# A weight-gradient matmul: where the halved output stores stand, and on which queues

## The chip, the cores and the metric

The kernel runs on one core of one Trainium2 chip. The metric is the device time of one execution in microseconds (us). The core has TensorE (PE in the profile, its weight loads PEld), VectorE (DVE), ScalarE (ACT), GpSimd (POOL) and SyncE (SP). SP, ACT and POOL can also issue DMA transfers, each on a queue of its own; the transfers run on 16 DMA engines.

## The reference

```python
batch, m, k, n = 16, 512, 1024, 768
grad_weight = np.einsum('bmk,bmn->kn', input, grad_output)   # float32 in and out
```

With batch and m taken together this is one product of a 1024 x 8192 matrix (X transposed) with an 8192 x 768 one (G); the result is 1024 x 768 floats, 3.1 MB.

## The kernel before, in words

The 8192 rows come in as 32 units of 256 rows, loaded by GpSimd and converted to bf16 on the way (lines 153 to 160). Only the first tiles are loaded as float32, by SP (L128, L130) and ScalarE (L129, L131), and rounded on VectorE and ScalarE (L202).

The result is cut in halves both ways: K into 0..511 and 512..1023, N into 0..383 and 384..767. Block A is the upper left quarter, B the upper right, C the lower left, D the lower right. Each has four pieces, q = 0 to 3, of 128 x 384 elements. The first four tiles are multiplied directly. For the other units a scheme with seven products in place of eight is used (Strassen's, in a form with few additions): the blocks 1, 5, 6, 7 are products of sums of quarters, made by VectorE (L184 to L198), and are added into A to D at the end. Running sums stand in SBUF (`acc` for A to D, `macc` for 1, 5, 6, 7) and visit PSUM banks: `fill` copies a sum into a bank (L309, ScalarE), `multiply` adds matmuls to it (L331), `close` brings it back (L356 on ScalarE; L360 to L378 on VectorE).

`PLAN` is a long string that fixes the order on TensorE, VectorE, ScalarE and GpSimd: `B2.1` is one matmul for block B, q = 2; `vB2` closes it on VectorE, `cC0` on ScalarE; `qA0` adds the shared block to A0 on GpSimd (L388, `add_shared`) and stores it; `pC1` adds it without a store. SP is not among the engines with a fixed order: the framework's scheduler orders the DMAs on SP's queue when the program is built.

Every piece of A to D is stored once, by `store` (L285 to L291): sixteen stores, all in the last 13 us, all issued by SP. A store of a piece is 128 rows of 384 floats (1536 bytes), 192 KB; half of one is 128 rows of 768 bytes, 96 KB. `stores[0]` counts the stores in the order of PLAN, and `HALVED = 4` makes the first four go out in two halves, one behind the other on SP. The end of PLAN, which holds most of the last sums:

```python
"51.2 vB3 f52@0 51.1 C0.1 pC1 C0.1 fB0@4 v51 C0.2 fB2@5 C1@2.4 vC0 B1.2 52.1 vC1 52.2 vB1 B2.3 v52 B2.2 "
"B0.4 vB2 B0.2 vB0 "
```

The last four stores are those of `vB1` (B1), `v52` (which also completes D2, L366 and L368), `vB2` (B2) and `vB0` (B0).

Before the first data arrive, TensorE runs dummy products (`WARMUP`, L134 to L142), all into one PSUM bank.

Of the kernel before, what the change touches and what calls it, by code (L numbers as in the profile page):

```python
# [9 lines left out]
P = 128  # L10
# [65 lines left out]
).split()  # L76

WARMUP = [("b", 512), ("f", 512), ("f", 512)] + 14 * [("b", 128)]
PAIRS_HELD = 11
SUMS_HELD = 8  # L80
MERGED = 2
HALVED = 4
ASIDES = 7
RESIDENT = 3
FOLDED = True
# [3 lines left out]
def kernel(  # L89
# [6 lines left out]
    nc = tc.nc  # L96
    bf16 = mybir.dt.bfloat16
    f32 = mybir.dt.float32
# [4 lines left out]
    NH = N // 2  # L103
# [4 lines left out]
    X = input.rearrange("b m k -> (b m) k")  # L108
    G = grad_output.rearrange("b m n -> (b m) n")
    OUT = out.rearrange("(ks p) n -> p ks n", p=P)  # L110
# [5 lines left out]
    psum = ctx.enter_context(tc.tile_pool(name="psum", bufs=1, space=bass.MemoryType.PSUM))  # L116
# [9 lines left out]
    xf = [pairs.tile([P, K], f32, name=f"xf{s}", tag="xp") for s in range(2)]  # L126
# [1 line left out]
    nc.sync.dma_start(out=gf[:, LEFT], in_=G[0:P, LEFT])  # L128
    nc.scalar.dma_start(out=xf[0], in_=X[0:P, :])  # L129
    nc.sync.dma_start(out=gf[:, RIGHT], in_=G[0:P, RIGHT])  # L130
    nc.scalar.dma_start(out=xf[1], in_=X[P : 2 * P, :])  # L131

    wps = psum.tile([P, 512], f32, name="bank7")
    for dt, cols in WARMUP:  # L134
        dtype = f32 if dt == "f" else bf16
        nc.tensor.matmul(
            wps[:, 0:cols],
            nc.const_aps.tensor(1.0, (P, P), dtype),
            nc.const_aps.tensor(1.0, (P, cols), dtype),
            start=True,  # L140
            stop=True,
        )  # L142
# [103 lines left out]
    def sum_of(p, q):  # L246
        if p in SLOT:
            return macc[:, SLOT[p], q, :]
        row = q if p in "AB" else Q + q
        return acc[:, row, LEFT if p in "AC" else RIGHT]  # L250
# [7 lines left out]
    prepared = set()  # L258
    opened = {(p, q): [] for p in streams for q in range(Q)}
    stores = [0]  # L260
# [21 lines left out]
    def last(p, q):  # L282
        return done[p, q] == len(streams[p])

    def store(p, q, c0, c1, engine):  # L285
        row = q if p in "AB" else Q + q
        at = 0 if p in "AC" else NH
        cuts = [c0, (c0 + c1) // 2, c1] if stores[0] < HALVED else [c0, c1]
        stores[0] += 1
        for d0, d1 in zip(cuts, cuts[1:]):  # L290
            engine.dma_start(out=OUT[:, row, at + d0 : at + d1], in_=sum_of(p, q)[:, d0:d1])  # L291

    asides = {(p, q): [] for p in streams for q in range(Q)}
    free_asides = list(range(ASIDES))
# [46 lines left out]
    def close(engine, p, q, queue):  # L341
        parts, carried = opened[p, q].pop(0)
        final = last(p, q) and not opened[p, q] and p not in ("1D" if FOLDED else "1")
        dst = sum_of(p, q)
        away = engine == "c" and not carried
        if away:
            assert not last(p, q)
            asides[p, q].append(free_asides.pop(0))
            dst = aside[:, asides[p, q][-1], :]
        for tile_, at, c0, c1 in parts:  # L350
            b = tile_[:, at : at + c1 - c0]
            to = dst[:, c0:c1]
            if engine == "c":
                assert carried or away
                assert not final or p in "ABC"
                nc.scalar.copy(out=to, in_=b)  # L356
            elif engine == "k":
                assert carried and not final and last("D", q) and not opened["D", q]
                d = sum_of("D", q)[:, c0:c1]
                (nc.vector.tensor_add if p == "C" else nc.vector.tensor_sub)(out=to, in0=b, in1=d)  # L360
                folded.add((p, q))
            elif final and p == "5":
                assert carried and {("6", q), ("7", q)} <= closed
                nc.vector.tensor_sub(out=to, in0=b, in1=sum_of("6", q)[:, c0:c1])  # L364
                d = sum_of("D" if FOLDED else "6", q)[:, c0:c1]
                nc.vector.tensor_sub(out=d, in0=b, in1=sum_of("7", q)[:, c0:c1])  # L366
                if FOLDED:
                    store("D", q, c0, c1, queue)  # L368
            elif final and (p, q) not in prepared:
                assert carried and (SHARED[p], q) in closed and (p != "D" or ("5", q) in closed)  # L370
                nc.vector.tensor_add(out=to, in0=b, in1=sum_of(SHARED[p], q)[:, c0:c1])  # L371
                if p in "BCD" and len(parts) == 2:
                    store(p, q, c0, c1, nc.sync if c0 == 0 else nc.scalar)
            elif carried:
                assert (p, q) not in prepared
                nc.vector.tensor_copy(out=to, in_=b)  # L376
            else:
                nc.vector.tensor_add(out=to, in0=b, in1=to)  # L378
        if final and p in "ABCD" and engine == "v" and (len(parts) == 1 or p == "A"):
            store(p, q, 0, NH, queue)  # L380
        if last(p, q) and not opened[p, q] and not (engine == "c" and p in "ABC"):
            closed.add((p, q))
        spilled.add((p, q))

# [12 lines left out]
    for token in PLAN:  # L397
        op, rest = token[0], token[1:]
        if op in "xg":
            stage, u = rest.split(".")  # L400
            (sum_x if op == "x" else sum_g)(int(stage), int(u))
        elif op == "r":
            round_by(*ROUNDINGS[int(rest)])
        elif op == "f":
            block, banks = rest.split("@")
            fill(block[0], int(block[1]), [int(b) for b in banks.rstrip("s").split("+")], banks.endswith("s"))
        elif op in "cvk":
            close(op, rest[0], int(rest[1]), nc.scalar if rest[2:] == "a" else nc.sync)
        elif op in "pq":
            add_shared(rest[0], int(rest[1]), op == "p", nc.scalar if rest[2:] == "a" else nc.sync)  # L410
        else:
            block, n = token.split(".")
            block, _, where = block.partition("@")
            multiply(block[0], int(block[1]), where, int(n))
# [34 lines left out]
```

## Time and profile before

| What | Value |
|---|---|
| Median of 3 runs | 161.4 us (161.18 to 161.44) |
| Profiled execution: its own time | 161.48 us |
| Profiled execution: span in the profile | 159.7 us |
| TensorE busy | 154.6 us (97%) |
| VectorE busy | 136.1 us (85%) |
| ScalarE busy | 104.4 us (65%) |
| GpSimd busy | 42.6 us (27%) |
| Granted TensorE clock | 0.999 |
| Stores: 12 of 192 KB, 8 of 96 KB | 2.1 and 1.7 us from issue to landing (medians) |

The span runs from the first to the last instruction of the profile; the execution's own time is 1.78 us longer. Times in the views are in us from the start of the span. L12 is line 12 of the kernel before.

### The profile page before, as it was taken

The numbers are of one execution on the slowest core, as the hardware profiler recorded it, in microseconds if no ns is written. First come the engines' busy times: TensorE is split into PE (matmuls) and PEld (weight loads), VectorE is DVE, ScalarE is ACT, GpSimd is POOL, SyncE is SP. The second block draws the span as 40 slices with busy tenths as digits, with TensorE's granted clock in tenths as the row PEclk, the third lists the DMA queues.
The fourth block names the chain that finished last, engine by engine and source line by source line (L and its number), as shares of the span: only waits on it lengthen the run. The fifth ranks groups of instructions, "written<-read, shape, count | busy, mean of one in ns | idle before, by whom it ended". The sixth has DMA issues, their size and how long they took to land.

```text
span 159.7 us, 2734 instructions
## 1 busy us (share of the span) xinstructions
PE 154.6 (97%) x931; PEld 91.2 (57%) x931; DVE 136.1 (85%) x316; ACT 104.4 (65%) x243; POOL 42.6 (27%) x77
## 2 busy tenths in 40 slices
PE   8899999999999999999999999999999999999990
PEld 3456656556555565665656565656566565656560
DVE  0514169999999999999999999989999899999992
ACT  3445238999999999967867585563465472339930
POOL 7442222222212222221222221222222100006930
PEclk9999999999999999999999999999999999999999
DMA  5999999999999999999999999999999999940696
GB/s 171 297 212 211 214 216 212 213 213 212 213 213 211 214 212 213 214 211 214 213 214 212 214 213 214 212 211 213 213 211 219 208 214 213 213 81 0 196 353 239
DMA packets 12829, 33.40 MB, mean 209 GB/s; under 512 B 1424, under 2 KB 4624, under 8 KB 12816
## 3 DMA queue, kind: packets, MB, share of 16 engines
q0 software_dynamic: 9360, 28.64, 90.7%
q1 hardware_dynamic: 3168, 3.54, 6.6%
q10 hardware_dynamic: 288, 1.05, 1.7%
q8 instruction: 7, 0.11, 0.3%
q14 instruction: 6, 0.05, 0.1%
HBM read 58.72 MB, written 3.15 MB: 387 GB/s over the span
## 4 chain that ended last, share of the span: by engine, by line
PE 91%; DMA 4%; DVE 2%; issue 1%; ACT 0%; ACTq 0%; DVEq 0%
PE bank L331 91%; DMA xf<-in_input_dram 4%; DVE acc L371 1%; DVE macc L364 0%; DVE xp L202 0%; ACT macc L356 0%; ACTq L129 0%; DVE acc L378 0%; DVE acc L366 0%; DVEq L371 0%
## 5 line engine op out<-in xcount | busy, mean ns | idle before, releaser
L331 PE MATMUL bank<-gp,xp 128*128 128x384 bf16 x576 | 105.4, 326 | 0.7 <-DVE xp L202 0.6
L331 PEld LDWEIGHTS <-xp 128*128 128x128 bf16 x576 | 55.8, 98 | 39.1 <-DVE xp L202 1.0
L331 PE MATMUL bank<-ge,xe 128*128 128x384 bf16 x336 | 65.9, 326 | 0.0
L331 PEld LDWEIGHTS <-xe 128*128 128x128 bf16 x336 | 32.7, 98 | 22.3 <-DVE xe L184 0.6
L309 ACT COPY bank<-macc 128x384 f32<-128x384 f32 x69 | 32.6, 489 | 10.4 <-DVE macc L378 6.2
L356 ACT COPY macc<-bank 128x384 f32<-128x384 f32 x64 | 29.4, 484 | 10.4 <-PE bank L331 10.1
L378 DVE TENSOR_TENSOR macc<-bank,macc 128x384 f32<-128x384 f32 x56 | 30.5, 554 | 1.2 <-PE bank L331 0.9
L154 POOL DMA_DIRECT2D xp<-in_input_dram x30 | 15.9, 529 | 52.6 <-DMA xp<-in_input_dram 21.9
L309 ACT COPY bank<-acc 128x384 f32<-128x384 f32 x46 | 21.8, 485 | 11.5 <-DVE acc L378 8.9
L356 ACT COPY acc<-bank 128x384 f32<-128x384 f32 x44 | 20.7, 480 | 11.4 <-PE bank L331 11.1
L153 POOL DMA_DIRECT2D gp<-in_grad_output_dram x30 | 15.9, 531 | 38.4 <-PE bank L331 17.2
L378 DVE TENSOR_TENSOR acc<-bank,acc 128x384 f32<-128x384 f32 x42 | 22.8, 553 | 1.9 <-PE bank L331 1.9
L184 DVE TENSOR_TENSOR xe<-xp 128x1024 bf16<-128x1024 bf16 x28 | 19.3, 689 | 1.0 <-DMA xp<-in_input_dram 0.9
L194 DVE TENSOR_TENSOR ge<-gp 128x768 bf16<-128x768 bf16 x28 | 15.5, 552 | 0.2 <-DMA gp<-in_grad_output_dram 0.2
L376 DVE COPY acc<-bank 128x384 f32<-128x384 f32 x9 | 5.0, 555 | 8.9 <-PE bank L331 8.9
L186 DVE TENSOR_TENSOR xe<-xe,xp 128x512 bf16<-128x512 bf16 x28 | 11.8, 421 | 0.3
L188 DVE TENSOR_TENSOR xp<-xp,xe 128x512 bf16<-128x512 bf16 x28 | 11.5, 419 | 0.0
L196 DVE TENSOR_TENSOR ge<-gp,ge 128x384 bf16<-128x384 bf16 x28 | 9.9, 353 | 0.2
L198 DVE TENSOR_TENSOR gp<-ge,gp 128x384 bf16<-128x384 bf16 x28 | 9.8, 354 | 0.2
L388 POOL TENSOR_TENSOR acc<-acc,macc 128x384 f32<-128x384 f32 x7 | 6.8, 1003 | 0.5 <-ACT acc L356 0.5
L388 POOL TENSOR_TENSOR macc<-macc 128x384 f32<-128x384 f32 x1 | 1.0, 1042 | 18.0 <-DVE macc L378 18.0
L202 DVE CAST gp<-gf 128x192 bf16<-128x192 f32 (+1 forms) x2 | 0.6, 310 | 4.9 <-DMA gf<-in_grad_output_dram 4.9
(23 smaller groups left out, 41.2 us busy)
## 6 DMA issues: line engine op xcount, KB each, us to landing
xp<-in_input_dram POOLq DMA_DIRECT2D x30, 512.0 KB, 16.7
gp<-in_grad_output_dram POOLq DMA_DIRECT2D x30, 384.0 KB, 16.7
out_dram<-acc SPq DMA_DIRECT2D x12, 192.0 KB, 2.1
xf<-in_input_dram ACTq DMA_DIRECT2D x2, 512.0 KB, 4.9
out_dram<-acc SPq DMA_DIRECT2D x8, 96.0 KB, 1.7
gp<-in_grad_output_dram POOLq DMA_DIRECT2D x3, 192.0 KB, 6.4
xp<-in_input_dram POOLq DMA_DIRECT2D x2, 256.0 KB, 7.8
gf<-in_grad_output_dram SPq DMA_DIRECT2D x2, 192.0 KB, 4.1
```

Of the source, the lines that this page charges most:

```text
L153: nc.gpsimd.dma_start(out=gp, in_=G[rows, :].rearrange("(p m) n -> p m n", m=2))
L154: nc.gpsimd.dma_start(out=xp, in_=X[rows, :].rearrange("(p m) k -> p m k", m=2))
L184: nc.vector.tensor_sub(out=xe[:, 0:2, :], in0=x[:, 1::-1, :], in1=x[:, 3::-2, :])
L186: nc.vector.tensor_sub(out=xe[:, 2, :], in0=xe[:, 0, :], in1=x[:, 0, :])
L188: nc.vector.tensor_add(out=x[:, 1, :], in0=x[:, 2, :], in1=xe[:, 2, :])
L194: nc.vector.tensor_add(out=ge[:, 0:2, :], in0=g[:, 0:2, :], in1=g[:, 1::2, :])
L196: nc.vector.tensor_add(out=ge[:, 2, :], in0=g[:, 3, :], in1=ge[:, 0, :])
L198: nc.vector.tensor_add(out=g[:, 1, :], in0=ge[:, 2, :], in1=g[:, 2, :])
L309: nc.scalar.copy(out=tile_[:, at : at + c1 - c0], in_=src[:, c0:c1])
L331: nc.tensor.matmul(tile_[:, at : at + c1 - c0], stat, mov[:, c0:c1], start=fresh, stop=True, skip_group_check=True,)
L356: nc.scalar.copy(out=to, in_=b)
L378: nc.vector.tensor_add(out=to, in0=b, in1=to)
```

## The change

The flag `HALVED` becomes a range of store numbers and is empty: the first four stores go out whole. A new tuple, `SHARED_STORES`, names stores 12 to 15, the last four: they are cut in two, the left half is issued by the queue that the store was given (SP), the right half by ScalarE. Stores are still 20 DMAs, 16 on SP and 4 on ScalarE in place of 20 on SP. Beside that, the first dummy product writes bank 4 and the others bank 7; the load of the second X tile can be cut in parts, with `X1_PARTS = 1` meaning one, as before; and `close` can end a prepared block of A, B or C on ScalarE, which no token of PLAN asks for. PLAN is the same.

```diff
-WARMUP = [("b", 512), ("f", 512), ("f", 512)] + 14 * [("b", 128)]
+WARMUP = [("b",512),("f",512),("f",512)]+14*[("b",128)]
...
-HALVED = 4
+X1_PARTS = 1
+HALVED = range(0)
+SHARED_STORES = (12,13,14,15)
...
-    nc.scalar.dma_start(out=xf[1], in_=X[P : 2 * P, :])
-
-    wps = psum.tile([P, 512], f32, name="bank7")
-    for dt, cols in WARMUP:
+    if X1_PARTS == 1:
+        nc.scalar.dma_start(out=xf[1], in_=X[P : 2 * P, :])
+    else:
...
+    warm = [psum.tile([P, 512], f32, name=f"bank{b}") for b in (4, 7)]
+    for n, (dt, cols) in enumerate(WARMUP):
         dtype = f32 if dt == "f" else bf16
         nc.tensor.matmul(
-            wps[:, 0:cols],
+            warm[min(n, 1)][:, 0:cols],
...
     def store(p, q, c0, c1, engine):
         row = q if p in "AB" else Q + q
         at = 0 if p in "AC" else NH
-        cuts = [c0, (c0 + c1) // 2, c1] if stores[0] < HALVED else [c0, c1]
+        n = stores[0]
         stores[0] += 1
+        middle = (c0 + c1) // 2
+        cuts = [c0, middle, c1] if n in HALVED or n in SHARED_STORES else [c0, c1]
         for d0, d1 in zip(cuts, cuts[1:]):
-            engine.dma_start(out=OUT[:, row, at + d0 : at + d1], in_=sum_of(p, q)[:, d0:d1])
+            by = nc.scalar if n in SHARED_STORES and d0 == middle else engine
+            by.dma_start(out=OUT[:, row, at + d0 : at + d1], in_=sum_of(p, q)[:, d0:d1])
...
+                assert (p, q) not in prepared or (final and carried and len(parts) == 1)
                 nc.scalar.copy(out=to, in_=b)
...
+        if final and engine == "c" and (p, q) in prepared:
+            store(p, q, 0, NH, queue)
-        if last(p, q) and not opened[p, q] and not (engine == "c" and p in "ABC"):
+        if last(p, q) and not opened[p, q] and (engine != "c" or p not in "ABC" or (p, q) in prepared):
```

More of the change, by code (lines that the diff above doesn't have):

```diff
@@ L130 @@
     nc.sync.dma_start(out=gf[:, RIGHT], in_=G[0:P, RIGHT])
-    nc.scalar.dma_start(out=xf[1], in_=X[P : 2 * P, :])
-    wps = psum.tile([P, 512], f32, name="bank7")
-    for dt, cols in WARMUP:
+    if X1_PARTS == 1:
+        nc.scalar.dma_start(out=xf[1], in_=X[P : 2 * P, :])
+    else:
+        n = P // X1_PARTS
+        for b in range(X1_PARTS):
+            engine = nc.scalar if b % 2 == 0 else nc.sync
+            engine.dma_start(out=xf[1][b * n : (b + 1) * n, :], in_=X[P + b * n : P + (b + 1) * n, :])
+    warm = [psum.tile([P, 512], f32, name=f"bank{b}") for b in (4, 7)]
+    for n, (dt, cols) in enumerate(WARMUP):
         dtype = f32 if dt == "f" else bf16
         nc.tensor.matmul(
-            wps[:, 0:cols],
+            warm[min(n, 1)][:, 0:cols],
             nc.const_aps.tensor(1.0, (P, P), dtype),
```

## The prediction

> **What bounds the kernel now.** I read the chain of waits on the page first, then the tail, because the diff touches only stores.
>
> ```profile
> ## 4 chain that ended last, share of the span: by engine, by line
> PE 91%; DMA 4%; DVE 2%; issue 1%; ACT 0%; ACTq 0%; DVEq 0%
> ```
>
> TensorE is 91% of the path, and no instruction of it is touched. The chain stops at VectorE's last sum, which starts at 156.12 and takes 0.56, so it ends at 156.68. The span is 159.7. The 3.0 us between hold only the last stores and the end barrier. The waits of SP's queue say who ends that stretch:
>
> ```profile
> SPq L444 <- DMA out_dram<-acc: 1.3, 3, 0.5
> ```
>
> At the end SP waits for stores to land, three of them in turn. The windows view, cut where one store's 192 KB give way to the next, says why (the last three columns are TensorE's clock, the DMA engines' busy share and GB/s):
>
> ```profile
> 148.00:149.93 1.93, 1.93 (x14) 1.15 (x13) 1.93 (x5) 1.93 (x6) 1.93 (x3) 1.00 0.64 204
> 149.93:151.85 1.92, 1.92 (x13) 1.15 (x12) 1.92 (x6) 1.92 (x6) 1.75 (x3) 1.00 0.65 205
> 151.85:152.41 0.56, 0.56 (x6) 0.36 (x4) 0.56 (x3) 0.56 (x3) 0.56 (x2) 1.00 0.99 354
> 152.41:152.94 0.53, 0.53 (x5) 0.32 (x4) 0.53 (x2) 0.53 (x2) 0.53 (x1) 1.00 1.02 365
> 152.94:156.16 3.22, 3.14 (x20) 1.66 (x17) 3.20 (x8) 0.17 (x1) 0.17 (x1) 1.00 1.03 366
> 156.16:158.38 2.22, 0.00 (x0) 0.00 (x0) 0.52 (x1) 0.00 (x0) 0.00 (x0) 1.00 0.99 354
> ```
>
> Up to 151.85 the eight halves of the first four stores go out, and the DMA engines are busy 64%: each half takes 0.48 us (98.3 KB at 204 GB/s). From 151.85 the twelve whole stores keep the engines full (0.99 to 1.03) until 158.4. At 366 GB/s one takes 196.6/366 = 0.537 us, and 151.86 + 12 x 0.537 = 158.3. So the tail is bound by the DMA engines' own time, not by SP's issuing, which is a little faster (below).
>
> **The change, part by part.** I call a store by its block: A0 is block A, q = 0. The built program gives SP's order before as A0 A2 A1 D3 C3 D0 A3 C2 B3 D1 C0 C1 B1 D2 B2 B0.
>
> *First four stores whole.* Eight issues on SP become four. The full stretch begins with C3, whose sum GpSimd ends at 149.01 + 1.97 = 150.98; SP issues at 151.00, and the engines fill at 151.86, 0.86 later (their share is 0.01 from 151.80 to 151.85 and 0.58 in the next 0.05 us). SP had finished the last half at 150.87 and was waiting for GpSimd already. So the saving is hidden by GpSimd's sums, and if that cover were gone it would be worth at most the 0.13 us between 150.87 and 151.00. I count 0.
>
> ```profile
> 149.01 1.97 POOL L388 TENSOR_TENSOR acc<-acc,macc 128x384 f32<-128x384 f32 x2
> 151.00 0.35 SPq L291 DMA_DIRECT2D out_dram<-acc  x1
> 151.45 0.39 SPq L291 DMA_DIRECT2D out_dram<-acc  x1
> 151.15 1.96 POOL L388 TENSOR_TENSOR acc<-acc,macc 128x384 f32<-128x384 f32 x2 [0.17 <-ACT acc L356]
> ```
>
> *SP's order.* SP is not in the hand-written schedule, and the changed program puts C2 before A3. C2 waits for GpSimd's add, which ends at 151.15 + 1.00 = 152.15; A3, whose sum VectorE ends at 150.86 + 0.55 = 151.41, is now queued behind that wait, and B3 (151.79 + 0.55 = 152.34) behind it. C2 is issued at 152.18 and reaches the engines 0.86 later, at 153.04. They are done with C3 and D0 at 152.94. Cost: 0.09 us idle, with 0 as the lower end. Behind that, SP issues every 0.49 us (151.45 to 152.42 is two issues), faster than the engines' 0.537, so nothing else runs dry.
>
> *Last four stores in two halves.* B1, D2, B2, B0 become eight 96 KB transfers inside the full stretch. What a half costs the engines is read from the first windows: 0.64 share at 204 GB/s is 196.6/204 x 0.64 = 0.617 us of engine time for two halves; a whole store takes 0.537 x 1.03 = 0.553. At the same overlap (1.03) the pair takes 0.60 us, 0.062 more; times four, 0.25. Before, the same penalty lay on the first four stores, where the engines had 36% to spare; now it lies where they have none. Bounds for the pair: 0.577 (+0.16 in all) at the share of 1.07 that I find when two hardware queues are active (2.90 to 3.40, below), 0.623 (+0.35) at the 0.99 of the last window.
>
> *Issuing the last pairs in parallel.* ScalarE made its last copy at 152.23 + 0.89 = 153.12, so its four issues wait for nothing but VectorE's sums, and behind them it has only the closing drain. B0 is ready at 156.68 and was issued at 156.70; both halves can go then and reach the engines at 157.56. The engines come to B0 only at 151.95 + 8 x 0.537 + 3 x 0.60 = 158.05. The 0.4 us of issue time that the second queue takes off SP are therefore hidden. The built program has SP's half of B0 wait for the semaphore that C1's store used. C1 landed 2.3 us after 154.41, at 156.7, and will land some 0.3 later; the half then reaches the engines near 157.95, still ahead of its turn. That margin, some 0.3 us for SP's half (it comes second), is the cover.
>
> *Warm-up and the rest.* The first dummy product writes bank 4 in place of 7. TensorE's order and waits are the same in both programs, and it later idles 0.62 us until 7.70 for the second X tile, which hides any shift. X1_PARTS = 1 takes the old branch; the new close() cases do not occur in this PLAN. 0.
>
> Sum: 0.25 + 0.09 = 0.34. The profiled span of 159.7 becomes 160.04, its time of 161.48 becomes 161.82. The median is 161.40, 0.08 below the profiled run, so I forecast **161.74**. The bounds (0.16 + 0 and 0.35 + 0.09) give 161.56 to 161.84 for this case.
>
> **Rival 1: both queues pass one unit that takes 0.48 us per transfer (much slower).** SP's halves never went faster than one per 0.48 us. If ScalarE's halves queued in the same place, from C1 (reaching the engines near 155.45) there would be eight more steps of 0.48 and a last half of 0.31: 155.45 + 3.84 + 0.31 = 159.60, against 158.30 by the same count before: +1.30, or 162.70. At 0.41 a step (two issues took 0.82) it is +0.74, or 162.14. It decides from 0.30 us a half upwards. For it: the packet records show the first packet of ScalarE's L129 at 2.28, 0.53 after SP's first at 1.76, though both issues began together. Against it:
>
> ```profile
> 0.74 0.37 SPq L128 DMA_DIRECT2D gf<-in_grad_output_dram  x1
> 1.17 0.43 SPq L130 DMA_DIRECT2D gf<-in_grad_output_dram  x1
> 0.74 0.41 ACTq L129 DMA_DIRECT2D xf<-in_input_dram  x1
> 1.18 0.46 ACTq L131 DMA_DIRECT2D xf<-in_input_dram  x1
> ```
>
> Four issues ended within 0.90 us, and neither queue's second was stretched by the other's first. [...]
>
> **Rival 2: two queues drain faster than one (faster).**
>
> ```profile
> 2.90:3.40 0.50, 0.50 (x2) 0.30 (x1) 0.00 (x0) 0.05 (x1) 0.50 (x2) 1.00 1.07 428
> ```
>
> Here SP's and ScalarE's loads share the engines and reach 428 GB/s. If the last four pairs did so, each would take 0.459: 4 x (0.537 - 0.459) = 0.31 gained, less 0.09, is -0.22, or 161.18. The floor is B0's sum: a lone half lands 1.6 to 1.7 us after its issue, B0 2.1, so no more than about 0.45 can be gained: 160.95. Against it: half of those packets are 4 KB, and the share of 1.07 is only 4% over 1.03, which is the 0.577 already counted.
>
> **Numbers.** Forecast 0.58; rival 1 0.16; rival 2 0.20; 0.06 for what I do not see, to either side. Some 0.2% (0.32 us, just over the 0.26 us spread of the three runs) can be told from no change; that bound is 161.72, so the forecast's range lies on both sides of it: 0.31 slower, 0.27 same. Rival 1 is slower; rival 2 gives 0.14 faster, 0.06 same. With the rest: faster 0.17, same 0.33, slower 0.50. For the range I take the forecast's and most of rival 2's, and rival 1's up to the middle of its prices: 161.0 to 162.4, which leaves out about 0.19 (half of rival 1, the floor of rival 2, the unseen).
>
> **What would show it.** Right: from 153 on the share near 1.0, four pairs at some 0.60 us, the engines done 0.3 later than 158.4, B0's halves landing near 159.1. The order step is wrong if no dip shows near 153.0. Rival 1 shows as a share of 0.64 after 156; rival 2 as more than 366 GB/s there. The whole reading is wrong if the engines idle before B0's halves arrive.

## The result, and the profile after

The changed kernel takes 161.93 us (median of 7, 161.68 to 162.12), the kernel before 161.36 us (7 runs): ratio 1.0035, 95% interval 1.0022 to 1.0047, that is +0.57 us (+0.36 to +0.76). The forecast was 161.74, with 161.56 to 161.84 for the forecast's own case; the median lies 0.09 us above that, and inside the range of 161.0 to 162.4 that also covers the rivals. The profiled execution of the changed kernel took 161.68 us, with a span of 159.8 us.

In that execution VectorE's last sum ended at 156.36 against 156.68 before, a scatter of the long TensorE part (rest_only below, with the stores of before, has 156.35). So I compare the tails from there: 159.81 - 156.36 = 3.45 us against 3.03 before, +0.42 us. The windows view of the changed kernel, cut at the first packets of the stores (the last three columns are the clock, the DMA engines' share and GB/s):

```profile
151.50:152.06 0.56, 0.56 (x6) 0.33 (x4) 0.56 (x3) 0.56 (x3) 0.56 (x2) 1.00 0.98 351
152.06:152.67 0.61, 0.61 (x5) 0.35 (x4) 0.61 (x2) 0.61 (x2) 0.61 (x1) 1.00 0.90 322
152.67:152.70 0.03, 0.03 (x3) 0.03 (x1) 0.03 (x1) 0.03 (x1) 0.03 (x1) 1.00 0.04 0
152.70:155.40 2.70, 2.70 (x18) 1.63 (x17) 2.70 (x7) 0.08 (x1) 0.08 (x1) 1.00 1.02 364
155.40:155.94 0.54, 0.36 (x3) 0.00 (x0) 0.52 (x2) 0.00 (x0) 0.00 (x0) 1.00 1.00 359
155.94:158.54 2.60, 0.00 (x0) 0.00 (x0) 0.41 (x1) 0.00 (x0) 0.00 (x0) 1.00 1.00 304
```

The second and third rows are the dip that the swapped order leaves: the share falls to 0.90 while D0 runs out (it was 1.02 there before), and to 0.04 just before C2's first packet. The last row is the four split stores: 2.60 us, where the last four took 2.28 before (156.16 to 158.45). Its 304 GB/s include the end, at which the engines run dry (a share of 0.80 from 158.10 to 158.54). So the rows to compare are those that stop short of it, first for before and then for the changed kernel:

```profile
156.16:158.00 1.84, 0.00 (x0) 0.00 (x0) 0.52 (x1) 0.00 (x0) 0.00 (x0) 1.00 1.02 366
```
```profile
155.94:158.10 2.16, 0.00 (x0) 0.00 (x0) 0.41 (x1) 0.00 (x0) 0.00 (x0) 1.00 1.04 316
```

The engines are as full as before, and move 316 GB/s in place of 366: a pair of halves takes 196.6/316 = 0.622 us, a whole store 0.537.

The issue rows of SP and ScalarE, D2's pair and then B0's (timeline), and the landings of B0's halves:

```profile
155.34 0.39 SPq L302 DMA_DIRECT2D out_dram<-acc  x1
155.34 0.37 ACTq L302 DMA_DIRECT2D out_dram<-acc  x1
156.39 0.34 ACTq L302 DMA_DIRECT2D out_dram<-acc  x1
156.54 0.33 SPq L302 DMA_DIRECT2D out_dram<-acc  x1
...
out_dram<-acc ACTq DMA_DIRECT2D x1, 96.0 KB, 2.3
out_dram<-acc SPq DMA_DIRECT2D x1, 96.0 KB, 2.4
```

D2's two issues start together and neither is stretched. B0's half on SP starts 0.15 us after ScalarE's; SP's waits name the cause, the landing of C1's store, whose semaphore it uses again (the second row; the first is SP's closing waits):

```profile
SPq L458 <- DMA out_dram<-acc: 1.6, 6, 0.4
...
SPq L302 <- DMA out_dram<-acc: 0.2, 1, 0.2
```

A half of B0 needs 2.3 to 2.4 us from issue to landing; the whole B0 of before needed 2.1.

### The profile page after: what moved, and what is told of

The parts are those of the page before. It is cut to its first block, busy times and chain, and to the rows that moved or that the text cites. A ratio compares the mean times of both kernels' runs of the same rounds, so it can differ in the third digit from the quotient of the medians.

```text
span 159.8 us, 2736 instructions
## 1 busy us (share of the span) xinstructions
PE 153.6 (96%) x931; PEld 91.2 (57%) x931; DVE 136.1 (85%) x316; ACT 104.3 (65%) x243; POOL 42.5 (27%) x77
## 4 chain that ended last, share of the span: by engine, by line
PE 91%; DMA 4%; DVE 2%; issue 1%; ACT 0%; ACTq 0%; DVEq 0%
PE bank L342 91%; DMA xf<-in_input_dram 4%; DVE acc L383 1%; DVE macc L376 0%; DVE xp L210 0%; ACT macc L368 0%; ACTq L131 0%; DVE acc L390 0%; DVE acc L378 0%; DVEq L383 0%
```

## The experiments

Theory 1 is the prediction's: with the DMA engines full, the swapped order and the smaller packets each cost engine time. Theory 2 lays the loss on the second queue itself, theory 3 on the rest of the diff. All kernels but three start from the kernel before; rest_only, split_on_sp_alone and sp_in_order_split start from the changed one. The table gives the time against the kernel before in the same session (medians 161.40 to 161.42 there), and three stretches of the profiled executions, from the DMA packet records and semaphore events of the trace, one execution of each kernel: from the first packet of C3 (of D0 in the sp_in_order kernels) to the last packet of all; from the end of VectorE's last sum to that last packet (both count packets that carry data); and from the last landing to the end of the span.

| Kernel | Median us | Ratio (95% interval) | Full stretch | Last sum to last packet | Landing to end |
|---|---|---|---|---|---|
| before | 161.36 | 1 | 6.59 | 1.77 | 0.91 |
| changed | 161.93 | 1.0035 (1.0022 to 1.0047) | 7.03 | 2.19 | 0.91 |
| rest_only | 161.30 | 0.9994 (0.9985 to 1.0003) | 6.58 | 1.76 | 0.92 |
| all_whole | 161.74 | 1.0019 (1.0010 to 1.0027) | 6.70 | 1.86 | 1.15 |
| all_whole_pad | 161.66 | 1.0014 (1.0006 to 1.0023) | 6.68 | 1.85 | 0.90 |
| split_both_ends | 162.06 | 1.0039 (1.0028 to 1.0051) | 6.90 | 2.08 | 1.22 |
| split_rows | 162.51 | 1.0068 (1.0056 to 1.0080) | 7.35 | 2.53 | 1.15 |
| whole_two_queues | 161.31 | 0.9998 (0.9990 to 1.0007) | 6.60 | 1.77 | 0.91 |
| split_on_sp_alone | 162.81 | 1.0091 (1.0076 to 1.0106) | 8.01 | 3.17 | 0.91 |
| sp_in_order_pad | 161.16 | 0.9989 (0.9981 to 0.9998) | 6.92 | 1.59 | 0.90 |
| sp_in_order_split | 161.48 | 1.0009 (1.0000 to 1.0018) | 7.15 | 1.81 | 0.97 |
| sp_in_order | 161.38 | 0.9997 (0.9988 to 1.0006) | 6.93 | 1.59 | 1.16 |

**rest_only: all but the stores**

```diff
-HALVED = range(0)
-SHARED_STORES = (12,13,14,15)
+HALVED = range(4)
+SHARED_STORES = ()
```

> All of the change but the stores: warm-up in two banks and the new branches, with the first four stores halved on SP as before. Theory 1 (small packets plus SP's order make the loss): no difference, within 0.1 us of before; from VectorE's last sum to the end of the span 3.0 us as before. Theory 3 (the warm-up's second bank, which shifts the PSUM banks, makes part of the loss): +0.1 to +0.2 us, with the tail still 3.0 us and the loss before the last sum.

No difference from before, and the same three stretches. The warm-up's second bank and the new branches are out of it; theory 3 falls.

**all_whole: the early halves taken away, nothing else**

```diff
-HALVED = 4
+HALVED = 0
```

> The kernel before with HALVED = 0: sixteen whole stores on SP, nothing on ScalarE. The built program has C2 ahead of A3 on SP, as in the changed kernel. Theory 1: only the 0.09 us in which the engines wait for C2 is lost: +0.09 us, tail about 3.1 us, and the last four stores take 0.537 us each. Theory 2 (the loss comes from the second queue alone): 0.00. A view in which SP's early issues bound the tail would have it faster by some 0.1 us.

+0.31 us by the ratio (the medians are 0.34 apart), of which the full stretch explains 0.11: the dip behind D0 is there again (windows view, cut at C2's first packet):

```profile
151.88:153.03 1.15, 1.15 (x9) 0.69 (x7) 1.15 (x4) 1.15 (x4) 1.15 (x2) 1.00 0.95 339
153.03:153.07 0.04, 0.04 (x3) 0.03 (x1) 0.04 (x1) 0.04 (x1) 0.04 (x1) 1.00 0.27 77
153.07:156.30 3.23, 3.06 (x19) 1.64 (x17) 3.21 (x8) 0.09 (x1) 0.09 (x1) 1.00 1.02 364
156.30:158.58 2.28, 0.00 (x0) 0.00 (x0) 0.42 (x1) 0.00 (x0) 0.00 (x0) 1.00 0.96 346
```

The last four take 2.28, as before. The rest of the loss, which no theory had, lies behind the last landing: 1.15 us to the end in place of 0.91. Sixteen stores use the eight completion semaphores in another phase: the last store is on the fourth of them, and SP's closing waits take them in a fixed order, so that four waits of about 0.06 us still follow its landing. In the changed kernel, with twenty store DMAs as before, the last to land has the last semaphore.

**all_whole_pad: the same with the phase restored**

```diff
-HALVED = 4
+HALVED = 0
...
     nc.scalar.dma_start(out=xf[1], in_=X[P : 2 * P, :])
+    pad = accp.tile([P, 4, 4], f32, name="pad")
+    for i in range(4):
+        nc.sync.dma_start(out=pad[0:16, i, :], in_=G[0:16, 0:4])
```

> As all_whole (HALVED = 0), which took 0.31 us more than before where the engines lost only 0.11: its last store landed 0.36 us after its last packet, as before, but 1.15 us passed from there to the end of the span where it is 0.91 before. Sixteen stores instead of twenty end on another of the eight completion semaphores, and SP's closing waits take them in a fixed order. This kernel adds four 256-byte loads into an unused tile on SP at the start, so that the last store has the last semaphore again. Theory 1 with the closing waits: +0.1 us against before (0.2 less than all_whole), landing to end 0.91. If the extra 0.25 us came from anything else in whole stores: +0.3 us as all_whole.

Landing to end is 0.90 again. SP's first closing drain (source view of L444, L447 here; first and last start stand behind the durations) shows it: for before, all_whole and all_whole_pad,

```profile
L444 SPq DRAIN  x3: 7/7/7, 158.9 to 159.2; - x3
```
```profile
L444 SPq DRAIN  x3: 7/7/7, 159.3 to 159.6; - x3
```
```profile
L447 SPq DRAIN  x3: 7/7/7, 159.1 to 159.4; - x3
```

with the last landings at 158.80, 158.94 and 158.98: 0.1, 0.4 and 0.1 us later. In the trace this kernel is 0.08 us behind before, from the last sum on. The timed difference of +0.25 (interval of the ratio: +0.10 to +0.37) is more than that, and no run here explains the rest; against all_whole, run in another session, the median fell by 0.08 where 0.2 was expected. So the closing waits are shown by the traces, and the times of these two kernels do not confirm their size. sp_in_order below, with and without the small loads, is a second test.

**split_both_ends: the split alone, in SP's old order**

```diff
-        cuts = [c0, (c0 + c1) // 2, c1] if stores[0] < HALVED else [c0, c1]
+        n = stores[0]
         stores[0] += 1
+        middle = (c0 + c1) // 2
+        cuts = [c0, middle, c1] if n < HALVED or n >= 12 else [c0, c1]
         for d0, d1 in zip(cuts, cuts[1:]):
-            engine.dma_start(...)
+            by = nc.scalar if n >= 12 and d0 == middle else engine
+            by.dma_start(...)
```

> The kernel before with the first four stores still halved on SP, and the last four in halves on SP and ScalarE as in the changed kernel. SP's order is that of before (A3 ahead of C2). Theory 1: the small packets alone, 4 x 0.062 to 4 x 0.08: +0.25 to +0.33 us, tail 3.3 to 3.4 us, no dip of the DMA share near the third store. If SP's order were the larger part: +0.1 or less.

```profile
151.64:155.96 4.32, 4.23 (x27) 2.35 (x24) 4.30 (x11) 1.26 (x4) 1.26 (x2) 1.00 1.02 364
155.96:158.54 2.58, 0.00 (x0) 0.00 (x0) 0.50 (x1) 0.00 (x0) 0.00 (x0) 1.00 0.99 305
```

No dip, and the last four take 2.58 us at 305 GB/s: the stretch is 0.31 us longer than before. That is theory 1's term, at its upper end. The time rose by 0.66, because with 24 store DMAs B0's halves have the third and fourth of the eight semaphores, and the half on the third lands last (158.89 against 158.71): five closing waits follow it, landing to end is 1.22, another 0.31. So all_whole's 0.11 and this kernel's 0.31 of engine time make 0.42, and the changed kernel's stretch is 7.03 - 6.59 = 0.44 longer: the two terms are the whole of it, within the 0.02 us by which they miss. (before, rest_only and whole_two_queues, which should have the same stretch, lie between 6.58 and 6.60.)

**whole_two_queues: the second queue without small packets**

```diff
+        by = nc.scalar if n in (13, 15) else engine
...
-            engine.dma_start(...)
+            by.dma_start(...)
```

> The kernel before, first four stores halved on SP, but of the last four, still whole, D2 and B0 go on ScalarE's queue. The count of DMAs, the order on SP and the packets of 1536 bytes stay. Theory 1 (the halves cost by packet size, the second queue neither helps nor harms): 0.00, within 0.05 us, packets at 66 ns, the last four in 2.28 us. Rival 2 (two queues drain faster): -0.1 us or more. Two queues disturb each other: +0.1 us or more.

```profile
151.85:156.17 4.32, 4.23 (x27) 2.35 (x24) 4.30 (x11) 1.27 (x4) 1.26 (x2) 1.00 1.01 364
156.17:158.45 2.28, 0.00 (x0) 0.00 (x0) 0.51 (x1) 0.00 (x0) 0.00 (x0) 1.00 0.95 345
```

Nothing moves, to 0.01 us. With whole stores the second queue neither drains the engines faster (rival 2) nor disturbs them (theory 2).

**split_rows: the second queue with halves of rows**

```diff
+            if n < 12:
...
+            else:
+                for by, r in ((engine, slice(0, 64)), (nc.scalar, slice(64, P))):
+                    by.dma_start(out=OUT[r, row, at + d0 : at + d1], in_=sum_of(p, q)[r, d0:d1])
```

> As the kernel before, but the last four stores are cut by rows: rows 0 to 63 go on SP, 64 to 127 on ScalarE, so the two queues work side by side with packets of 1536 bytes as in a whole store. Theory 1 (packet size): the loss is all but gone, +0.00 to +0.04 us. Theory 2 (two queues that share the engines disturb each other, or a unit behind both takes 0.3 us and more a transfer): as large as with column halves, +0.25 us and more.

Both missed: +1.11 us, of which about 0.24 are closing waits (24 store DMAs, the last to land on the fourth semaphore). The packets have 1536 bytes, but the engines deliver less than with column halves: 260 GB/s at a share of 0.88, where split_both_ends has 305 at 0.99. The four issues on SP take 0.53 to 0.79 us each, and with the waits between them span 2.84 us, where those of the changed kernel span 2.12:

```profile
155.94:158.96 3.02, 0.00 (x0) 0.00 (x0) 0.49 (x1) 0.00 (x0) 0.00 (x0) 1.00 0.88 260
...
154.66 2.84 SPq L296 DMA_DIRECT2D out_dram<-acc  x4
```

A transfer of 64 rows is another thing than half of one with 128, so this run does not separate packet size from queue; whole_two_queues and the next kernel do. Why 64 rows are so slow stays open; it also means that the length of a packet is not the only thing that sets the pace of a store here.

**split_on_sp_alone: the changed kernel with both halves on SP**

```diff
-            by = nc.scalar if n in SHARED_STORES and d0 == middle else engine
+            by = engine
```

> The changed kernel with the right halves on SP too: the same twenty DMAs, the same packets, one queue. If each issuing queue has its own 0.48 us per transfer (as I read the four rows at the start): from C1's first packet eight steps of 0.48 and a half of 0.43, some 0.9 us more than the changed kernel, +1.3 us against before. If both queues pass one unit (rival 1): the same as the changed kernel, +0.55 us.

```profile
152.79:156.02 3.23, 3.05 (x19) 1.63 (x17) 3.21 (x8) 0.09 (x1) 0.09 (x1) 1.00 1.02 364
156.02:156.76 0.74, 0.00 (x0) 0.00 (x0) 0.42 (x1) 0.00 (x0) 0.00 (x0) 1.00 0.89 270
156.76:159.60 2.84, 0.00 (x0) 0.00 (x0) 0.00 (x0) 0.00 (x0) 0.00 (x0) 0.70 0.65 208
```

+1.40 us against before, and a full stretch 0.98 longer than the changed kernel's. In the third row one queue feeds halves at its own pace: 98.3 KB at 208 GB/s is one per 0.47 us, with the engines 35% idle, as the early halves went in the kernel before. With ScalarE's queue beside it eight halves took 2.60 us, 0.33 each. So the pace of 0.47 belongs to the one queue, and rival 1 falls at its prices. (A shared unit of some 0.32 us a half would give the changed kernel's time as well, but then the engines would wait for it, and their share was 1.04 until 158.10.) The second row, where the engines still had work from C1, gives 270 GB/s at a share of 0.89, 303 at a full one: the 304 of the changed kernel, from one queue. The changed kernel's 316 GB/s at 1.04 are 304 at a full share too. So the small packets cost the same with one queue as with two.

**sp_in_order_pad, sp_in_order_split, sp_in_order: what the reading predicts in the other direction**

```diff
-    ctx.enter_context(tc.manual_schedule(engines={E.PE, E.DVE, E.Activation, E.Pool}))
+    ctx.enter_context(tc.manual_schedule(engines={E.PE, E.DVE, E.Activation, E.Pool, E.SP}))
```

with HALVED = 0, and in the first with the four small loads; in the second the line is put into the changed kernel and nothing else. SP then issues in the program's order, D0 ahead of C3 and A3 ahead of C2.

> Whole stores on SP with the four small loads of all_whole_pad, and SP added to the engines whose order is the program's: D0 (ready 0.50 us ahead of C3) goes ahead of C3 and A3 ahead of C2. Theory 1 (the tail is the engines' 0.537 us a store from the first store of a full stretch on): the stretch begins with D0, 0.49 us earlier, and is then held a little by B1 to B0 becoming ready; B0's packets end 0.18 us earlier than before: -0.2 us, 161.2. If the end is set by VectorE's last sum alone: 0.00.

> The changed kernel with SP in the program's order (D0 ahead of C3, A3 ahead of C2) and nothing else; twenty DMAs, so the last store has the last semaphore without the small loads. If the two terms add up: the order term turns from +0.1 into a start of the full stretch 0.5 us earlier than before, and the halves still cost 4 x 0.08. D2 is ready too late to use all of the early start: packets end 1.8 us after VectorE's last sum (1.77 before, 2.19 in the changed kernel, 1.59 with whole stores in order): about 161.4, 0.0 against before. If the halves only cost where the engines are behind, and the early start frees them: as sp_in_order_pad, -0.2 us.

> sp_in_order_pad without the four small loads. Closing waits: the last store is on the fourth of the eight completion semaphores again, four more waits of some 0.06 us follow its landing, landing to end 1.15 us: +0.25 us against sp_in_order_pad, 161.4. If the small loads changed the time in another way: 161.2.

sp_in_order_pad takes 161.16 us, ratio 0.9989 (0.9981 to 0.9998), a gain of 0.18 us (0.03 to 0.31) against before, only just clear of no change. Its stretch begins 5.33 us ahead of VectorE's last sum (4.82 before), and the last packet ends 1.59 us behind it (1.77 before), the 0.18 that was expected:

```profile
151.53:155.99 4.46, 4.46 (x30) 2.64 (x27) 4.46 (x11) 1.77 (x5) 1.76 (x2) 1.00 0.99 352
155.99:158.44 2.45, 0.27 (x2) 0.00 (x0) 0.85 (x2) 0.00 (x0) 0.00 (x0) 1.00 0.90 321
```

The share of 0.90 in the last four (0.96 before, up to its last packet) fits the expected new bound: the engines now wait a little for VectorE's sums. With the four pairs of halves (sp_in_order_split) the last packet is at 1.81, and the time is 161.48: the order is worth 0.4 us to the changed kernel, and the halves still cost 0.2 where little is left to hide them. Without the small loads (sp_in_order) the packets are the same, the landing to end is 1.16, and the time 161.38, as before (ratio 0.9997). That is 0.22 more than sp_in_order_pad, as four closing waits would have it; but the two were run in different sessions and the intervals of their ratios overlap, so here too it is the trace that shows the waits.

## Why the prediction was right, point by point

*The bound.* That the tail is engine time, and not SP's issuing, is shown from both sides: a second queue for whole stores changes nothing (a full stretch of 6.60 us against 6.59), and an earlier start of the full stretch brings the last packet 0.18 us forward, as expected.

*First four stores whole, counted 0.* C3's first packet stands 4.84 us ahead of VectorE's last sum (4.82 before). Right.

*SP's order, 0.09.* The dip is at its place, and the stretch of all_whole and all_whole_pad is 0.09 to 0.11 longer. Right in size. Most of it is not the idle gap that the prediction counted (0.03 to 0.04 us long) but the falling share in front of it, while D0's last packets drain.

*Halves, 0.25.* Right in kind, small in size: 0.31 in the stretch of split_both_ends, 0.32 in the last four of the changed kernel. The engine time of a half came from windows in which the engines had 36% to spare (204/0.64 = 319 GB/s at a full share). With the engines full it is 304, and the trace's 768-byte packets take 38 to 39 ns (medians) where they took 36; why they take longer there, no run shows. The overlap of 1.03 was right (1.04), and so was a whole store's 0.537. A pair took 0.622, where 0.60 was forecast: just inside the upper bound of 0.623.

*Parallel issue hidden; SP's half of B0 held by C1's landing.* SP's half was issued 0.15 us behind ScalarE's, where the prediction had some 0.4 (157.95 against 157.56), and the engines stayed full (1.04). Both hidden, as said.

*Warm-up, 0.* rest_only: right.

*The sum.* 0.34 forecast, 0.42 in the profiled tails, 0.57 (0.36 to 0.76) timed. The tails lie inside the bounds that the prediction gave its own sum (0.16 to 0.44), at their upper end; the median does not (161.93 against 161.84), and is inside the range only because that was stretched for the rivals, so that much is luck. The 0.15 between the tails and the median lies inside the interval, and no run here names a cause for it.

*Rival 1.* Wrong: D2's two issues, which start together, ran side by side (0.39 and 0.37 us, no longer than the others there, 0.33 to 0.44), and the same halves on one queue took 0.9 us more. The rival's time was 162.14 to 162.70, against the 161.93 measured. The price itself was good for one queue: split_on_sp_alone took 162.81. The late first packet of L129, which spoke for it, stays unexplained.

*Rival 2.* Wrong: whole_two_queues moved nothing, and the pairs on two queues went at 316 GB/s, not above 366.

## What to carry to other kernels

Where the DMA engines were full up to the end, a second issuing queue gained nothing (whole_two_queues: ratio 0.9998) and halves at the end cost time: 0.31 us of engine time for four pairs in split_both_ends. They belong, if anywhere, where the engines have time to spare: the early halves, which left them 36% idle, did not delay the full stretch (C3's first packet 4.82 us ahead of VectorE's last sum with them, 4.84 without). First look when the full stretch starts and whether a store that is ready stands behind one that is not: putting SP's queue in the order of readiness moved the last packet forward by 0.18 us here. And a change in the number of DMAs can shift which completion semaphore the last one uses, which is a cost of its own: landing to end was 1.16 us in sp_in_order and 0.90 in sp_in_order_pad, and the 0.26 between them is more than that gain. Count the DMAs before crediting a difference to the edit.

## What the runs showed of the hardware that was not expected

- SP's closing waits on the eight completion semaphores take about 0.06 us each, in a fixed order, also for those that are long complete (in the kernel before, four of them for transfers that had landed 0.7 to 2.1 us earlier). Landing to end goes with the place of the semaphore whose transfer lands last: 0.90 to 0.92 us for the eighth, 0.97 for the seventh (sp_in_order_split), 1.15 to 1.16 for the fourth, 1.22 for the third (split_both_ends).
- On SP's queue alone, 96 KB halves went at one per 0.47 to 0.48 us (204 to 208 GB/s, the engines 35% idle), hardly faster than the 0.49 us at which SP issues whole stores of twice the size. Two queues together fed one half per 0.33 us, with the engines full.
- Stores of 64 rows moved worse than stores of half the columns: 260 GB/s at a share of 0.88, and issues of 0.50 to 0.79 us in place of 0.33 to 0.44. The cause was not tried.
